# Stick-breaking fill by block count, the second recurrence's values projected before the first recurrence's queries, first gate blocks after the second recurrence's inputs

## The chip, the cores and the metric

One NeuronCore of a Trainium2 chip runs the whole kernel. The metric is device time in microseconds of that core, from start to end of one execution. Five engines work side by side: PE (TensorE, the matmuls), DVE (VectorE), ACT (ScalarE), POOL (GpSimd) and SP (SyncE, which here only issues DMAs). Each engine takes its own instructions strictly in order, and waits on semaphores where it needs another engine's result.

## What is computed

One decoder layer over 1024 tokens of width 1024. A projection `x @ w_in` yields the inputs of three causal mixers, each 256 wide with 4 heads: A, stick-breaking attention; B, a gated linear recurrence (HGRN2); C, another (GLA). Their outputs are normed, gated, projected up, weighted by sigmoid gates, summed, projected once more and layer-normed.

```python
# A: stick-breaking, per head, blocks of 128 queries against all keys before them
z = q @ k.T * scale
log_one_minus = where(s < t, log_sigmoid(-z), 0)
tail = reverse_cumsum(log_one_minus) - log_one_minus
a_out = masked_exp(s < t, log_sigmoid(z) + tail) @ v
# B and C: S_t = diag(f_t) S_{t-1} + k_t^T v_t ; o_t = S_t^T q_t
# merge
merged = sum_n sigmoid(x @ w_gate[n]) * (y[n] @ w_up[n])
out = layer_norm(ALPHA * x + merged @ w_out)
```

## The kernel before

All matmuls take their operands split into a high and a low part, so each product is three passes. A projection of 128 output channels over half of the tokens (`proj_T`, L207) is 24 matmuls with 512 columns; a projection of 256 channels for 128 tokens (`proj_N`, L220) is 24 matmuls with 256 columns.

The program is written as **chains** and a **stream**. Five chains run one after the other, and each is a long sequence of dependent small steps: the two stick-breaking units `c_sb(0)` and `c_sb(1)` (two heads each), then `c_rec` for GLA, for HGRN heads 0 and 1 (`("H", 0)`), and for heads 2 and 3 (`("H", 1)`). The stream is an ordered list of generators with all the plain projections, which depend on little. After each step a chain yields a number, which is added to a budget; the loop then draws pieces of the stream (each piece says what it costs, mostly 1.3 for six 512-column matmuls or twelve 256-column ones) until the budget is used up. Before a chain starts, `need(label)` draws whatever the chain still lacks, without any chain step between. A generator whose input does not exist yet yields 0.0, and that ends the drawing for this step: so `f_split(0)` (`ys0`) blocks the stream until the second stick-breaking unit has ended, and `f_finish(C_G, ...)` (`("y", 2)`) blocks it until the GLA chain has ended.

**Stick-breaking.** A unit has 24 chunks, each 128 queries against 1 to 4 blocks of 128 keys, 72 blocks in all. `weights` (L548) does two matmuls, two sigmoids on ACT, masks on POOL, a scan (L570) and a product (L571) on DVE. Three chunks later `transposed` (L577) turns the result over on PE (L586) and splits it (`ath` on ACT, `atl` on DVE, helper lines L98 and L99); `values` (L594) multiplies with V (L608). After `weights` and after `transposed` the unit yields `SB_T * 0.5`, which is 0.8 for a chunk of any width.

**Recurrence.** `c_rec` starts with small products (L645), fills of the score tiles `sc` on POOL (L662) and then seven levels h = 1 to 64, each for two halves of the tokens. In the GLA chain a half of a level copies Q into block-diagonal form (ACT, L675), takes its low part (DVE, L678, 8 instructions), splits K (tile `Kp`), does 12 matmuls (L694), copies the masked scores (DVE L703, up to h = 16; ACT after that; level 1 uses L670) and scales Q and K (DVE, L716 and L717). It yields `R4_T` = 3.4 per half of a level. After the levels come transposes of K (`kn`), the states (L745 to L753), the outputs (L765, L767, tiles `og`) and the norms (to L782).

**Stream pieces that matter here.** `f_cv` (`fC`), `f_ag` and `f_ck` project GLA's values, the gate of A and GLA's keys. `f_cq` (`GLA`) projects GLA's queries and multiplies them out on DVE and ACT (L406 to L409: the product, its three bf16 parts `prod`). `f_hi` (`vH`, L324) projects the values of both HGRN chains: eight `proj_N` and two ACT copies each, into four tiles. `f_h(0)` projects forget gate and queries of the first HGRN chain, 96 matmuls, with DVE work like that of `f_cq` (L419 to L437). `f_gate(0, True, 0, 2)` (`g0`) does the first two of eight gate blocks of branch A: per block and half 24 matmuls, a sigmoid into a `gt` tile, 6 matmuls with `ys0`'s split `yh`, `yl` (L505) and one DVE product into a tile `mT` (L508).

**Order of execution.** The program order is a priority, not the order on the engines. A scheduler lays out each engine's queue ahead of time: it takes the earliest instruction in program order whose inputs, by its own estimates, are there and whose output tile has a free buffer. Tiles come from pools with a fixed number of buffers; the ones here are `h` (29 buffers of 128x512 f32: `V`, `ks`, `kl`, `qs`, `vC`, `vH`, `K`, `Q`, `prod`, `yh`, `yl`, `mT`, `og` and others), `gt` (2: `gt`, the products before their split) and in PSUM `mm` (3, for all projections). A projection whose result has no free tile to go to keeps its `mm` buffer.

Of the kernel before, what the change touches and what calls it, by code (L numbers as in the profile page):

```python
# [32 lines left out]
PX = -3000000  # L33
NWO = 2
NWARM = 10
SB_T = 1.6
CV_T = 10.0
CV0 = 1
CV1 = 2
# [4 lines left out]
SB_LAG = 3  # L44
# [11 lines left out]
def hybrid_layer_kernel(ctx, tc, x, x_t, w_in, gla_gate_w2, gla_gate_b, hgrn_lb_logits,  # L56
# [276 lines left out]
    def f_cv():  # L333
        load_small()
        ws = load_w(W, C_V, 256, extra=C_R)
        vC = [H("vC", shape=[P, 2, 256]) for _ in range(4)]
        cr = sm.tile([P, 8, 16], F32, tag="cr", name="cr", bufs=1)
        for tt in range(8):
            pt = yield from proj_N(ws, tt, 272)
            nc.scalar.copy(vC[tt // 2][:, tt % 2, :], pt[:, 0:256])  # L340
            nc.vector.tensor_copy(cr[:, tt, :], pt[:, 256:272])
            yield 1.4
        d["vC"] = vC
        fs, xbs, nas = [[H(n) for _ in range(2)] for n in ("f", "xb", "na")]
        crT = [GT("crT", F32R) for _ in range(2)]

        def rank16():
            for th in range(2):
                c = crT[th]
                nc.gpsimd.memset(c[0:80].bitcast(F32), 0.0)  # L350
                pt = ptr()
                for j in range(4):
                    nc.tensor.transpose(pt[0:16, j * P:(j + 1) * P], cr[:, th * 4 + j, :], ident)
                nc.scalar.copy(c[0:16], pt[0:16])
                nc.vector.tensor_tensor(c[32:48], pt[0:16], c.bitcast(F32)[0:16], op=ALU.subtract)
                nc.scalar.copy(c[64:80], pt[0:16])
            later.append([CV1, up])

        def up():
            for th in range(2):  # L360
                xb, na = xbs[th], nas[th]
                pt = ptr()
                mm(pt, w2s[0:80], crT[th][0:80], start=True, stop=True)
                nc.vector.tensor_scalar(xb, pt, gb, None, op0=ALU.add)
                nc.vector.scalar_tensor_tensor(na, xb, -1.0, xb, op0=ALU.mult, op1=ALU.min)
                nc.vector.tensor_scalar(xb, xb, 0.0, None, op0=ALU.min)
            later.append([CV2, decay])

        def decay():

            lower_bound()
            with at_priority(PW):
                for na, xb in zip(nas, xbs):
                    nc.scalar.activation(xb, xb, AF.Exp, scale=1.0 / 16)
                    nc.scalar.activation(na, na, AF.Exp)
                for na in nas:
                    nc.scalar.activation(na, na, AF.Ln, bias=1.0)
                for na in nas:
                    nc.scalar.activation(na, na, AF.Exp, scale=-1.0 / 16)
            for th in range(2):  # L380
                nc.vector.tensor_tensor(fs[th], xbs[th], nas[th], op=ALU.mult)
            d["fC"] = fs
            budget[0] += CV_T

        later.append([CV0, rank16])

    def f_ck():
        uk = load_w(W, C_QK + P, P)
        K = [H("K") for _ in range(2)]
        for th in range(2):  # L390
            pt = yield from proj_T(uk, th)
            nc.scalar.copy(K[th], pt)
            yield 1.3
        d["KC"] = K
# [141 lines left out]
    def c_sb(un):  # L536
        qs, ks, kl = d["qk", un]
        V = d["V"][un]
        oT = [H("oT") for _ in range(2)]
        chunks = []  # L540
        for hd in range(2):
            for jp in range(4):
                for g in reversed(range((2 * jp + 5) // 4)):
                    for ti in range(2):
                        chunks.append((hd, jp, g, ti))
        right, part, at, po = {}, {}, {}, {}

        def weights(c):  # L548

            hd, jp, g, ti = c  # L550
            i = jp * 2 + ti
            ni = min(4, i + 1 - 4 * g)
            cw = ni * P
            cm = max(cw, 256)
            last = 4 * g + ni == i + 1
            qq, th = qs[hd][i // 4], slice((i % 4) * P, (i % 4 + 1) * P)
            be, om = R("be"), R("om")
            pt = pz()
            mm(pt[:, 0:cm], qq[:, th], ks[hd][g][:, 0:cm], start=True, stop=False)
            mm(pt[:, 0:cm], qq[:, th], kl[hd][g][:, 0:cm], start=False, stop=True)  # L560
            nc.scalar.activation(om[:, 0:cw], pt[:, 0:cw], AF.Sigmoid, scale=-0.125)  # L561
            nc.scalar.activation(be[:, 0:cw], pt[:, 0:cw], AF.Sigmoid, scale=0.125)
            if last:

                for a_, fill in ((om, 1.0), (be, 0.0)):
                    nc.gpsimd.affine_select(a_[:, cw - P:cw], a_[:, cw - P:cw], [[-1, P]], compare_op=ALU.is_gt, fill=fill,  # L566
                                            base=0, channel_multiplier=1)
            rv = om[:, 0:cw][:, ::-1]
            rt = right.get((hd, i))
            nc.vector.tensor_tensor_scan(rv, rv, rv, 1.0 if last else rt[:, 0:1], op0=ALU.mult, op1=ALU.bypass)  # L570
            nc.vector.tensor_tensor(be[:, 0:cw - 1], be[:, 0:cw - 1], om[:, 1:cw], op=ALU.mult)  # L571
            if not last:
                nc.vector.tensor_tensor(be[:, cw - 1:cw], be[:, cw - 1:cw], rt[:, 0:1], op=ALU.mult)
            right[hd, i] = om
            part[c] = (be, ni)

        def transposed(c):  # L577
            hd, jp, g, ti = c
            be, ni = part.pop(c)
            ns = min(4, 2 * jp + 2 - 4 * g)  # L580
            if ti == 0:
                at[hd, jp, g] = (S("ath", F32R, [P, 4, 256]), S("atl", F32R, [P, 4, 256]))
            ath, atl = at[hd, jp, g]
            pt = ptr([P, 4, P])
            for j in range(ni):
                nc.tensor.transpose(pt[:, j, :], be[:, j * P:(j + 1) * P], ident)  # L586
            ts = slice(ti * P, (ti + 1) * P)
            split(ath[:, 0:ni, ts], atl[:, 0:ni, ts], pt[:, 0:ni, :])
            if ni < ns:

                for a_ in (ath, atl):
                    nc.vector.tensor_scalar(a_[:, ni, ts], ident, 0.0, None, op0=ALU.mult)

        def values(c):  # L594
            hd, jp, g, ti = c
            if ti == 0:
                return
            hr, otr = ((rA, rB), (rB, rA))[hd]
            nst = 2 * jp + 2
            ns = min(4, nst - 4 * g)  # L600
            if 4 * g + ns == nst:
                po[hd, jp] = pav()[:, 0:256]
            p_ = po[hd, jp]
            at_ = at.pop((hd, jp, g))
            for s in range(ns):
                v = V[2 * g + s // 2][:, s % 2, hd, :]
                for n, a_ in enumerate(at_):
                    mm(p_, v, a_[:, s, :], start=(4 * g + ns == nst and s == 0 and n == 0), stop=(g == 0 and s == ns - 1 and n == 1))  # L608
            if g == 0:
                tmp = R("ot")  # L610
                sl = slice(jp % 2 * 256, jp % 2 * 256 + 256)
                nc.scalar.copy(tmp[hr, 0:256], p_[otr])
                nc.vector.tensor_tensor(oT[jp // 2][hr, sl], p_[hr], tmp[hr, 0:256], op=ALU.add)

        n = len(chunks)
        for k in range(n + SB_LAG + 1):
            if k < n:
                weights(chunks[k])
                yield SB_T * 0.5
            if 0 <= k - SB_LAG < n:  # L620
                transposed(chunks[k - SB_LAG])
                yield SB_T * 0.5
            if 0 <= k - SB_LAG - 1 < n:
                values(chunks[k - SB_LAG - 1])
        need(("ag", un))
        for th in range(2):
            nc.vector.tensor_tensor(oT[th], oT[th], d["ag", un][th], op=ALU.mult)
        d.setdefault("ya", []).append(oT)
        if un == 1:
            d["y", 0] = d["ya"]  # L630

    def c_rec(key, nh, V):
# [139 lines left out]
        for i, o in enumerate(og):  # L772
# [12 lines left out]


    stream = [("V", f_av()), (("qk", 0), f_qk(0)), (("qk", 1), f_qk(1)), (("ag", 0), f_ag(0)),
              ("fC", f_cv()), (("ag", 1), f_ag(1)), ("KC", f_ck()), ("GLA", f_cq()),
              (("ys", 0), f_split(0)), ("g0", f_gate(0, True, 0, 2)), ("vH", f_hi()), (("H", 0), f_h(0)),
              (("y", 2), f_finish(C_G, gng, "ogC", ("y", 2))), (("H", 1), f_h(1)), ("g0", f_gate(0, True, 2, 8)),  # L790
              (("y", 1), f_finish(H_G, hng, "ogH", ("y", 1))), (("ys", 2), f_split(2)), ("g2", f_gate(2, False)),
              (("ys", 1), f_split(1)), ("g1", f_gate(1, False, 0, 7)), ("wo", f_wout(range(NWO))), ("g1", f_gate(1, False, 7, 8))]
# [44 lines left out]
    for label, mk in chains:  # L837
        need(label)
        for t_fill in mk():
            budget[0] = max(budget[0], -3.0) + t_fill  # L840
            while budget[0] > 0:
                c = advance()
# [104 lines left out]
```

## Time and profile before

| | us |
|---|---|
| median of 3 runs (lowest, highest) | 838.28 (837.74, 839.07) |
| profiled execution | 838.19 |
| its span, first to last instruction | 836.3 |
| PE busy | 813.9 |
| DVE busy | 500.6 |
| ACT busy | 352.0 |
| POOL busy | 138.2 |

The profiled execution is 1.9 us longer than its span, and lies 0.1 us under the median. The two stick-breaking units run from 54 to about 129 and on to about 214 us, the GLA chain to about 335, the HGRN chains to about 455; gate blocks and the output projection fill the rest. A busy PE is not a PE at its peak, as matmuls overlap: six 512-column matmuls follow each other in 1.39 us though each shows some 0.4 us.

### The profile page before, as it was taken

The numbers are of one execution on the slowest core, as the hardware profiler recorded it, in microseconds if no ns is written. First come the engines' busy times: TensorE is split into PE (matmuls) and PEld (weight loads), VectorE is DVE, ScalarE is ACT, GpSimd is POOL, SyncE is SP. The second block draws the span as 40 slices with busy tenths as digits, with TensorE's granted clock in tenths as the row PEclk, the third lists the DMA queues.
The fourth block names the chain that finished last, engine by engine and source line by source line (L and its number), as shares of the span: only waits on it lengthen the run. The fifth ranks groups of instructions, "written<-read, shape, count | busy, mean of one in ns | idle before, by whom it ended". The sixth has DMA issues, their size and how long they took to land.

```text
span 836.3 us, 12346 instructions
## 1 busy us (share of the span) xinstructions
PE 813.9 (97%) x4576; PEld 694.8 (83%) x4576; DVE 500.6 (60%) x1033; ACT 352.0 (42%) x733; POOL 138.2 (17%) x234
## 2 busy tenths in 40 slices
PE   8999999999899999999999999999999999999996
PEld 7987799787779989988888889888888888888886
DVE  6469998869999868667844224222232223266665
ACT  6466565696544737455645213221222222241110
POOL 3011212131400012312110002222222121210000
PEclk9999999999999999999999999999999999999998
DMA  9421110110010101100412211121212122142211
GB/s 263 116 54 26 26 26 2 45 45 26 14 38 27 52 25 27 44 20 20 132 33 82 58 50 39 35 60 35 61 33 63 34 60 65 43 126 101 100 51 51
DMA packets 66508, 46.22 MB, mean 55 GB/s; under 512 B 4352, under 2 KB 61328, under 8 KB 66448
## 3 DMA queue, kind: packets, MB, share of 16 engines
q1 hardware_dynamic: 65008, 42.36, 18.2%
q10 hardware_dynamic: 1440, 3.08, 1.0%
q8 instruction: 36, 0.59, 0.3%
q14 instruction: 24, 0.20, 0.1%
HBM read 41.23 MB, written 4.19 MB: 54 GB/s over the span
## 4 chain that ended last, share of the span: by engine, by line
PE 80%; DVE 11%; issue 4%; ACT 2%; POOL 1%; DMA 1%; SPq 0%; POOLq 0%; DVEq 0%; ACTq 0%
PE mm L207 40%; PE mm L220 12%; PE mm L879 11%; PE mm L505 7%; PE z L694 4%; DVE om L570 2%; PE av L767 2%; DVE atl L99 1%; PE av L608 1%; DVE Qlo L678 1%; DVE be L571 1%; PE av L765 1%; DVE wl L99 1%; PE z L745 1%; DMA xraw<-in_x_t_dram 1%
## 5 line engine op out<-in xcount | busy, mean ns | idle before, releaser
L207 PE MATMUL mm<-xh,wh 128*128 128x512 f32 x576 | 230.3, 400 | 0.0
L207 PE MATMUL mm<-xh,wl 128*128 128x512 f32 x576 | 228.7, 397 | 0.0
L207 PE MATMUL mm<-xl,wh 128*128 128x512 f32 x576 | 227.7, 395 | 0.0
L207 PEld LDWEIGHTS mm<-xh,wh 128*128 128x128 f32 x576 | 109.4, 190 | 23.0 <-DVE mT L508 0.4
L207 PEld LDWEIGHTS mm<-xh,wl 128*128 128x128 f32 x576 | 108.2, 188 | 24.0
L207 PEld LDWEIGHTS mm<-xl,wh 128*128 128x128 f32 x576 | 108.5, 188 | 22.5
L99 DVE TENSOR_TENSOR wl<-wr,wh 128x512 fp32r<-128x512 f32 (+2 forms) x116 | 74.5, 649 | 80.6 <-ACT wh L98 79.4
L98 ACT CAST wh<-wr 128x512 fp32r<-128x512 f32 (+2 forms) x116 | 66.4, 576 | 105.4 <-PE mm L207 92.9
L220 PE MATMUL mm<-wh,xh 128*128 128x256 f32 (+1 forms) x320 | 92.0, 287 | 0.4 <-ACT wh L98 0.3
L220 PE MATMUL mm<-wl,xh 128*128 128x256 f32 (+1 forms) x320 | 90.9, 284 | 0.7 <-DVE wl L99 0.7
L220 PE MATMUL mm<-wh,xl 128*128 128x256 f32 (+1 forms) x320 | 90.5, 283 | 0.0
L879 PE MATMUL mm<-wo,mh 128*128 128x512 f32 (+1 forms) x288 | 80.8, 366 | 0.0
L511 POOL TENSOR_TENSOR mT<-mT,gt 128x512 f32<-128x512 f32 x32 | 46.8, 1463 | 178.9 <-DVE gt L510 178.9
L510 DVE TENSOR_TENSOR gt<-mm,gt 128x512 f32<-128x512 f32 x32 | 22.1, 691 | 83.2 <-PE mm L505 82.9
L499 ACT ACTIVATE gt<-mm 128x512 f32<-128x512 f32 x48 | 28.6, 596 | 97.1 <-PE mm L207 92.1
L220 PEld LDWEIGHTS mm<-wh,xh 128*128 128x128 f32 x320 | 60.4, 189 | 1.6 <-ACT wh L98 1.3
L220 PEld LDWEIGHTS mm<-wl,xh 128*128 128x128 f32 x320 | 60.3, 188 | 1.3 <-DVE wl L99 1.3
L220 PEld LDWEIGHTS mm<-wh,xl 128*128 128x128 f32 x320 | 60.4, 189 | 0.4 <-DVE xl L99 0.2
L879 PEld LDWEIGHTS mm<-wo,mh 128*128 128x128 f32 x288 | 52.0, 189 | 9.1 <-DVE wo L99 0.4
L879 PE MATMUL mm<-wo,ml 128*128 128x512 f32 (+1 forms) x144 | 52.6, 366 | 0.0
L505 PE MATMUL mm<-yl,wh 128*128 128x512 f32 x96 | 38.2, 398 | 1.9 <-DVE yl L99 1.9
L566 POOL TENSOR_SCALAR_AFFINE_SELECT om<-om 128x128 f32<-128x128 f32 x32 | 13.3, 414 | 151.3 <-ACT om L561 146.8
(204 smaller groups left out, 1318.5 us busy)
## 6 DMA issues: line engine op xcount, KB each, us to landing
wr<-in_w_in_dram SPq DMA_DIRECT2D x92, 256.0 KB, 2.8
xraw<-in_x_t_dram SPq DMA_DIRECT2D x16, 256.0 KB, 5.6
xr<-in_x_dram SPq DMA_DIRECT2D x8, 512.0 KB, 3.3
wr<-in_w_out_dram SPq DMA_DIRECT2D x16, 256.0 KB, 2.9
wr<-in_w_up_dram SPq DMA_DIRECT2D x24, 128.0 KB, 2.2
out_dram<-xr SPq DMA_DIRECT2D x7, 256.0 KB, 2.1
out_dram<-xr ACTq DMA_DIRECT2D x7, 256.0 KB, 2.1
lng<-in_ln_g_dram ACTq DMA_DIRECT2D x1, 512.0 KB, 4.3
```

Source lines behind the costliest of these rows:

```text
L98: nc.scalar.copy(hi, src)
L99: nc.vector.tensor_tensor(lo, src, hi.bitcast(F32), op=ALU.subtract)
L207: mm(pt, w_, x_, start=(n == 0), stop=(n == 23))
L220: mm(pt, x_, w_, start=(n == 0), stop=(n == 23))
L499: nc.scalar.activation(gt, pt, AF.Sigmoid)
L505: mm(pu, w_, y_[th], start=(k == 0), stop=(k == 5))
L510: nc.vector.tensor_tensor(gt, pu, gt, op=ALU.mult)
L511: nc.gpsimd.tensor_tensor(mT, mT, gt, op=ALU.add)
L570: nc.vector.tensor_tensor_scan(rv, rv, rv, 1.0 if last else rt[:, 0:1], op0=ALU.mult, op1=ALU.bypass)
L694: mm(pt[:, wi * nh:(wi + 1) * nh], k_[:, w * P:(w + 1) * P], q.rearrange("p a (n h) -> p a n h", h=h), start=(n == 0 and wi == 0), stop=(n ...
L767: mm(pt[:, wi, a, :], sc[b][:, wi, a, :], V(w)[:, a * 64:a * 64 + 64], start=(w == 0 and a == 0), stop=True, skip_group_check=True)
L879: mm(pt, l_, r_[e][:, o:o + w], start=(n == 0), stop=(n == 23))
```

## The change

Three edits. The stick-breaking yields become `SB_T * 0.5` times the number of key blocks of the chunk, with `SB_T` at 0.6 instead of 1.6: 0.3 to 1.2 per yield where it was 0.8. In the stream, `vH` moves from behind the first two gate blocks to ahead of `f_cq` (`GLA`). And the first two gate blocks move from ahead of `("H", 0)` to behind it. Nothing that is computed changes.

```diff
-SB_T = 1.6
+SB_T = 0.6
@@
+        def blocks(c):
+            hd, jp, g, ti = c
+            return min(4, jp * 2 + ti + 1 - 4 * g)
+
         def weights(c):
             hd, jp, g, ti = c
             i = jp * 2 + ti
-            ni = min(4, i + 1 - 4 * g)
+            ni = blocks(c)
@@
                 weights(chunks[k])
-                yield SB_T * 0.5
+                yield SB_T * 0.5 * blocks(chunks[k])
             if 0 <= k - SB_LAG < n:
                 transposed(chunks[k - SB_LAG])
-                yield SB_T * 0.5
+                yield SB_T * 0.5 * blocks(chunks[k - SB_LAG])
@@
     stream = [("V", f_av()), (("qk", 0), f_qk(0)), (("qk", 1), f_qk(1)), (("ag", 0), f_ag(0)),
-              ("fC", f_cv()), (("ag", 1), f_ag(1)), ("KC", f_ck()), ("GLA", f_cq()),
-              (("ys", 0), f_split(0)), ("g0", f_gate(0, True, 0, 2)), ("vH", f_hi()), (("H", 0), f_h(0)),
+              ("fC", f_cv()), (("ag", 1), f_ag(1)), ("KC", f_ck()), ("vH", f_hi()), ("GLA", f_cq()),
+              (("ys", 0), f_split(0)), (("H", 0), f_h(0)), ("g0", f_gate(0, True, 0, 2)),
               (("y", 2), f_finish(C_G, gng, "ogC", ("y", 2))), (("H", 1), f_h(1)), ("g0", f_gate(0, True, 2, 8)),
```

## Rows read from the trace of the kernel before

**Rows 1.** The page, part 1: engine, busy us, share of the span, instructions.

```profile
PE 813.9 (97%) x4576; PEld 694.8 (83%) x4576; DVE 500.6 (60%) x1033; ACT 352.0 (42%) x733; POOL 138.2 (17%) x234
```

**Rows 2.** Windows: stretch, length, then busy us of PE, PEld, DVE, ACT, POOL.

```profile
54.00:129.00 75.00, 71.42 (x425) 61.29 (x424) 68.34 (x130) 47.44 (x105) 13.39 (x32) 1.00 0.10 26
129.00:182.00 53.00, 51.26 (x316) 44.69 (x315) 43.65 (x84) 39.11 (x79) 12.63 (x28) 1.00 0.11 28
182.00:214.00 32.00, 29.74 (x158) 23.81 (x157) 29.94 (x66) 21.68 (x48) 7.20 (x16) 1.00 0.11 29
214.00:234.00 20.00, 18.05 (x129) 14.44 (x127) 19.83 (x33) 9.31 (x21) 7.06 (x8) 1.00 0.14 38
234.00:279.00 45.00, 42.32 (x313) 39.84 (x314) 43.40 (x123) 22.27 (x62) 3.11 (x10) 1.00 0.07 20
279.00:298.00 19.00, 19.00 (x112) 16.76 (x111) 11.77 (x31) 13.83 (x32) 2.66 (x5) 1.00 0.26 70
298.00:335.00 37.00, 36.73 (x281) 33.10 (x281) 30.72 (x75) 19.47 (x35) 8.55 (x15) 1.00 0.09 22
335.00:398.00 63.00, 63.00 (x416) 56.93 (x415) 42.91 (x94) 31.43 (x65) 15.32 (x31) 1.00 0.10 28
...
829.00:836.30 7.30, 0.00 (x0) 0.00 (x0) 3.54 (x10) 0.75 (x2) 1.50 (x2) 0.61 0.20 72
```

**Rows 3.** Who waited for whom, PE: us in total, times, longest.

```profile
PE av L608 <- DVE atl L99: 3.8, 5, 1.5
PE mm L505 <- DVE yl L99: 1.9, 1, 1.9
...
PE z L694 <- DVE sc L703: 1.4, 2, 1.0
...
PE z L694 <- DVE Kp L99: 1.2, 2, 0.8
```

**Rows 4.** The chain of work in order of time: start, us, what.

```profile
74.18 1.39 PE mm L207 x6
...
257.48 1.43 PE z L694 x12
258.91 4.24 PE mm L220 x36
```

**Rows 5.** Groups of DVE instructions by shape: busy us, mean ns of one, idle before.

```profile
L99 DVE TENSOR_TENSOR wl<-wr,wh 128x512 fp32r<-128x512 f32 x88 | 60.8, 698 | 59.1 <-ACT wh L98 58.0 <-PE mm L207 0.6
L703 DVE COPY_PREDICATED sc<-mask,z 128x512 f32<-128x512 int32 x32 | 26.9, 868 | 4.3 <-PE z L694 4.2
L678 DVE TENSOR_TENSOR Qlo<-Q,Qbd 32x128 fp32r<-32x128 f32 x96 | 24.6, 289 | 2.0 <-ACT Qbd L675 1.4
...
L716 DVE TENSOR_TENSOR Q<-Q,G 128x256 f32<-128x256 f32 x36 | 15.3, 430 | 4.4 <-ACT Qbd L675 2.0 <-POOL St L735 1.3 <-POOL G L719 1.0
...
L670 DVE COPY_PREDICATED sc<-mask,r 128x512 f32<-128x512 int32 x8 | 11.6, 1476 | 0.7 <-POOL sc L662 0.7
...
L434 DVE TENSOR_TENSOR Q<-mm,s 128x512 f32<-128x512 f32 x4 | 2.8, 690 | 1.4 <-PE mm L207 1.0 <-PE av L765 0.4
```

**Rows 6.** One line's instructions: ns min/median/max, first and last start.

```profile
L406 DVE SCALAR_TENSOR_TENSOR Q<-mm,f x2: 680/684/689, 192.9 to 206.4; 128x512 f32<-128x512 f32 x2
...
L694 PE MATMUL z<-Qbd,Kp x96: 277/283/386, 233.6 to 293.8; 128*128 128x256 f32 x96
```

**Rows 7.** Tile prod: what its engines waited for, who waited for it (us, times).

```profile
  PE av L767: 9.8, 2
...
  PE av L765: 7.1, 3
...
  DVE mT L508: 4.0, 1
```

## The prediction

> **What bounds the kernel now.** I read the page's first part, then windows cut at the chains' borders, then who waited for whom, then single lines. The page shows PE busy for 97% and DVE for 60% [rows 1], which suggests that only PE counts. The windows correct that [rows 2]. From 335 us on PE is full, with matmuls back to back (63.00 of 63.00 in the window shown), and the change can only shift that part. From 54 to 335 us DVE is nearly as full as PE: 68.3 of 75 in the first stick-breaking unit, 73.6 of 85 in the second (two windows), 63.2 of 65 from 214 to 279. PE's idle time there is the length less the busy time of each window: 3.6, 1.7, 2.3, 1.9, 2.7, 0 and 0.3, together 12.5 us. Nearly all of its longer waits are on DVE results: `atl` 3.8, `yl` 1.9, `sc` 1.4, `Kp` 1.2 us [rows 3]. Only this 12.5 us can be won; all matmuls stay. What can be lost is any further time in which the stream has nothing to give while DVE works through a chain.
>
> Prices on PE: six 512-column matmuls 1.39 us, 36 of 256 columns 4.24 us, the 12 matmuls of half a level 1.43 us [rows 4]. So `vH` (192 of 256 columns) is 22.6 us of PE, `("H", 0)` (96 of 512) 22.2, a gate half (30) 7.0 and the four halves moved 27.8.
>
> **Fill by width.** One unit's yields sum to 72 x 0.6 = 43.2 instead of 24 x 1.6 = 38.4: 4.8 units are some 5 us more of PE work in each, moved, not added. Narrow chunks draw 0.6 instead of 1.6, full ones 2.4. DVE's work per chunk (scan, product, `atl`) grows with width as well, so the draws now lie where PE waits for `atl`. But DVE is 91% full in the first unit, and cannot be outrun: of the 3.6 us idle I keep 2 (bounds 0, all covered, and 5, the same waits with the narrow chunks bare).
>
> **`vH` ahead of `f_cq`.** Before, the second unit's budget takes the rest of `fC`, `ag`, `KC` and `GLA`, and the stream then stands at `ys0` for the last six yields. The scheduler still found work, the matmuls of `g0` that need no `y`. After, budget 43.2 + 10 (`CV_T`) buys the rest of `fC` (7 pieces), `ag` (8), `KC` (8), all 16 of `vH` and 3 of the 8 pieces of `f_cq`. The other 5 are drawn by `need("GLA")`. `vH` loads DVE lightly: its copies are ACT's, and its four weight pieces cost DVE 4 x 0.70 [rows 5]. `f_cq` costs DVE nine instructions per half, at most 0.69 each by the nearest row (L434) [rows 5], and these leave the unit. So DVE gets room there and the unit is bound by PE; of 4.0 us idle (129 to 214) I keep 2 (bounds 0 and 4). Its DMAs, four weight pieces on SP's queue ahead of two, move earlier; SP waits for nothing there that PE lacks.
>
> The price is that `f_cq` ends later. Its last product starts at 206.4 now [rows 6]; after, at 206.4 + 22.6 less some 2 us of saved idle, about 227. Everything in the GLA chain hangs on it. What was ahead of the chain on DVE, however, is not all delayed with it.
>
> **The GLA chain.** Now 27.2 us pass from that product to the first L694, and 60.2 more to the last [rows 6]. Its own DVE work, by count: L678 24.6 (96 of them, all GLA's), L703 16 of 32, so 13.9, L670 4 x 1.48 = 5.9, Q scaled 14 x 0.43 = 6.0, K about the same, `Kp` 12 splits at about 0.43 (taken from the 256-column L716) 5.2: 62 us [rows 5]. That is why DVE shows 43.4 of 45. Between product and first L694, `atl`, `yl` and gate products crowd DVE now; after, the unit's tail is done by then, and 12 to 16 us should do: first L694 at 239 to 243. Then the levels: beside them DVE now has the gates' products, `vH`'s and part of `("H", 0)`'s work; after, `("H", 0)` comes first, whose halves cost DVE more (a forget half three instructions, a query half nine, some 7 to 8 us per half in all). So the 60 us do not shrink: last L694 some 6 us later than now, and the levels done near 305 instead of 298.
>
> **What PE has meanwhile.** From 227 to 305 are 78 us. PE has the levels (12 x 1.43 = 17.2) and the fill that comes ahead of the block at `("y", 2)`: 22.2 + 27.8. The chain asks for 6.0 + 14 x 3.4 = 53.6 units, the stream has 20.8 + 26.0 = 46.8, and from level 64 on nothing is drawn until the chain ends; before it had 67.6 and ran out only in the outputs. If all the fill can run, PE idles 78 - 67.2 = 11 us, or 3 if `("y", 2)` runs ahead into its three PSUM buffers (72 matmuls, 8.5 us). But the last stage (298 to 335 now, 0.3 us idle) then lacks this fill and idles up to 8 more: lower bound 11. If it cannot run, it is because tiles are short. In the levels `h` holds `vC` 4, `K` 2, `Q` 2, `vH` 4, `yh`/`yl` 8 and the f and K tiles of `("H", 0)` 4, which is 24; its first query half takes 5, and all 29 are gone. The second needs 3, and the gate block's `mT` more. Then each `mm` buffer is held by a result without a tile, and only 54 gate matmuls (12.5 us) still run: PE idles 78 - 17.2 - 22.2 - 12.5 = 26, with 2 us of new waits 28, the upper bound. That such waits exist the trace shows: `prod` waited for the outputs' matmuls 9.8 and 7.1 us, and an `mT` product waited 4.0 us for a matmul that reads `prod` [rows 7]. But there the fill was not stopped for long. I take 17 from 214 us to the end of the chain, near the middle, where 4.9 us stand now. The 1.9 us on `yl` are among those 4.9: with the gates later that wait is gone.
>
> **Sum.** Idle now 12.5; after 2 + 2 + 17 = 21. On the profiled execution's 838.2 (span 836.3, where the last window ends [rows 2], and 1.9 around it; 0.1 under the median): 838.2 + 8.5 = 846.7. Ends: 0 + 0 + 11 gives 836.7, 5 + 4 + 28 gives 862.7.
>
> The Trainium skill (Perfetto Trace Analysis, section Optimization Strategy) says that a gap which repeats on the engine that should be full can mean that no SBUF or PSUM is left for the next tile. By that rule the upper bound of the GLA chain would hold. The trace agrees only as far as the `prod` and `mT` waits go; a stretch of repeating gaps it does not show.
>
> **Rivals.** (1) Faster, about 830. The units' 7.6 us of idle and the 1.9 on `yl` go, and the chain is no later: DVE has some 15 us of room in the second unit and uses it for the unit's tail and the first half of `f_cq`, so that the levels keep their end at 298. Then idle falls from 12.5 to about 4: 838.2 - 8.5 = 829.7. It decides if the first L694 starts by about 233. For it: each wait that the trace names is met by one of the edits. Against: DVE was gapless from 234 to 279 and PE's fill there becomes dearer for DVE. (2) Tiles run out throughout: 2 + 2 + 28 instead of 12.5, 857.7; the mark is `mm` held while `h` is full. (3) The change doesn't do what it says: as the scheduler draws by readiness, the moves cancel and idle stays at 12.5: 838.2. For it: gate matmuls already ran ahead of `ys0`.
>
> **Chances.** Forecast (841 to 853) 0.45, rival 1 0.33, rival 2 0.12, rival 3 0.10. A measurement of this kernel can tell about 0.2% (1.7 us) from no change. Faster 0.33, same 0.11, slower 0.56. The range must reach rival 1 and the lower of rival 2: 829 to 857.
>
> **What would show it.** Right: windows of the units with PE idle under 3 us each; last L406 near 227, first L694 near 240, last near 300; PE idle over 10 us between there and the end of the GLA chain, and no wait of L505 on `yl`. Wrong: a first L694 at 233 or earlier; PE full from 227 to 305, which would say that DVE's list was shorter than I count; idle over 5 us in a unit, which would say that narrow chunks were left bare. From the end of the GLA chain on the two traces should agree instruction by instruction.

## The result, and the profile after

The changed kernel takes 866.8 us (862.1 to 867.2), the kernel before, on the same chip, 838.1: a ratio of 1.033 (95%: 1.031 to 1.035). The direction was forecast, the size was not: 8.5 us were expected and some 28 came, more than the range's upper end and more than rival 2. Its four executions lie further apart than those of the kernel before (837.7 to 839.1): 862.1 at a mean granted clock of 0.986, and 866.5 to 867.2 at 0.978 to 0.983. In `c_sb` and `c_rec` the changed kernel's lines stand 4 further down (L694 is L698, L608 is L612, L728 is L732); up to L546 nothing has moved.

The profiled execution is 866.5 us, its span 864.7. The page's first part and two digit rows of its second (the span in 40 slices of 21.6 us), to be held against [rows 1]:

```profile
span 864.7 us, 12344 instructions
PE 828.2 (96%) x4576; PEld 703.7 (81%) x4576; DVE 506.9 (59%) x1033; ACT 348.7 (40%) x729; POOL 137.2 (16%) x234
PE   8999999999879689999899999999999999999996
PEclk9999999999989699999999999999999999999999
```

PE's instructions are the same 4576, yet its busy time rose by 14.3 us. Half of the loss sits inside what counts as busy, and the length less the busy time doesn't show it. The other half is idle: span less busy was 22.4 and is 36.5, so 14.1 more, and 14.3 + 14.1 are the span's 28.4. The windows of [rows 2] in after, and one more (stretch, length, then busy us of PE, PEld, DVE, ACT, POOL, then granted clock, DMA share, GB/s):

```profile
54.00:129.00 75.00, 72.34 (x438) 62.67 (x437) 67.63 (x129) 47.98 (x105) 13.53 (x32) 1.00 0.10 26
129.00:182.00 53.00, 50.65 (x309) 43.79 (x308) 40.57 (x83) 38.83 (x76) 11.12 (x22) 1.00 0.14 37
182.00:214.00 32.00, 31.15 (x252) 30.42 (x251) 26.39 (x50) 19.78 (x53) 6.24 (x15) 1.00 0.03 7
214.00:234.00 20.00, 17.39 (x103) 14.01 (x101) 16.31 (x28) 8.50 (x20) 5.52 (x12) 1.00 0.22 59
234.00:279.00 45.00, 38.92 (x205) 30.54 (x204) 43.08 (x86) 20.02 (x44) 9.11 (x12) 0.92 0.10 27
279.00:298.00 19.00, 13.07 (x53) 10.12 (x52) 16.92 (x52) 7.84 (x21) 0.83 (x4) 0.67 0.00 1
298.00:335.00 37.00, 33.17 (x153) 26.81 (x154) 23.17 (x68) 17.68 (x40) 4.48 (x10) 0.89 0.09 24
335.00:398.00 63.00, 63.00 (x464) 57.83 (x463) 40.72 (x90) 28.20 (x54) 11.08 (x17) 1.00 0.13 33
398.00:460.00 62.00, 59.63 (x379) 51.18 (x378) 39.55 (x83) 28.56 (x60) 11.14 (x26) 1.00 0.20 62
```

PE's idle time by stretch is 2.7, 2.4 and 0.9 in the units (7.6 before), 2.6, 6.1, 5.9 and 3.8 from 214 to 335 (4.9 before), and a new 2.4 after 398. Look at 279 to 298: PE ran 112 matmuls there before and 53 now, at a granted clock of 0.67. The groups of PE by shape (busy us with overlaps counted once, mean ns, idle before) show whose busy time grew:

```profile
L698 PE MATMUL z<-Qbd,Kp 128*128 128x256 f32 x96 | 26.8, 377 | 15.0 <-DVE Kp L99 12.0 <-DVE sc L707 1.0 <-ACT sc L702 1.0
...
L698 PE MATMUL z<-Qlo,Kp 128*128 128x256 f32 x48 | 12.3, 348 | 0.0
```

The kernel before shows 16.2 and 9.6 for these two groups, so they account for 13.3 of the 14.3 us. A matmul with no neighbour to overlap with shows its whole length, and one at a lower granted clock takes longer: in the timeline below a pair of these matmuls shows 0.40 us at 282.07 and 0.63 us at 286.78. PE's timeline shows the stretch (start, us, what, and in brackets the idle time before it and its releaser):

```profile
278.28 0.39 PE L505 MATMUL mm<-yh,wh 128*128 128x512 f32 x1
...
280.02 0.40 PE L505 MATMUL mm<-yh,wl 128*128 128x512 f32 x1
281.49 0.51 PE L698 MATMUL z<-Qbd,Kp 128*128 128x256 f32 x2 [1.07 <-DVE Kp L99]
281.83 0.40 PE L698 MATMUL z<-Qlo,Kp 128*128 128x256 f32 x2
282.07 0.40 PE L698 MATMUL z<-Qbd,Kp 128*128 128x256 f32 x2
...
285.76 0.80 PE L698 MATMUL z<-Qbd,Kp 128*128 128x256 f32 x2 [1.63 <-DVE Kp L99]
286.35 0.63 PE L698 MATMUL z<-Qlo,Kp 128*128 128x256 f32 x2
286.78 0.63 PE L698 MATMUL z<-Qbd,Kp 128*128 128x256 f32 x2
...
290.76 0.80 PE L698 MATMUL z<-Qbd,Kp 128*128 128x256 f32 x2 [1.32 <-DVE Kp L99]
...
312.12 0.50 PE L207 MATMUL mm<-xh,wh 128*128 128x512 f32 x1 [0.30 <-DVE prod L435]
```

From 281.5 to 308.7 PE runs 80 L698 and nothing else, at first 12 in 5 us. Five times a half of a level waits for DVE's `Kp` (1.07 to 1.63 us); the last ones wait for ACT's copies of the scores. No stream piece runs between the last L505 at 280.0 and the L207 at 312.1. By then 504 L207 and 6 L505 had run since the start: 480 L207 are all that the stream lists ahead of the gates (the second half of `("H", 0)`'s queries among them), so 24 L207 and 6 L505 belong to the gates, and the gates then stood still.

What they stood for is on DVE. Its timeline where the stretch ends:

```profile
310.78 0.69 DVE L434 TENSOR_TENSOR Q<-mm,s 128x512 f32<-128x512 f32 x1 [0.91 <-PE tr L732]
311.38 0.68 DVE L435 TENSOR_TENSOR prod<-mm,s 128x512 f32<-128x512 f32 x1
...
327.08 0.69 DVE L508 TENSOR_TENSOR mT<-mm,gt 128x512 f32<-128x512 f32 x1 [5.85 <-PE tr L732]
```

L434 takes `("H", 0)`'s second query half out of its `mm` buffer. None of its inputs comes from L732, the transposes that read GLA's K, so what it waited for was the buffer of its result `Q`, which those reads set free; and the L207 at 312.1 waited for its `mm` buffer in turn. The first `mT` product, L508, waited for L732 as well. A second pool stood in the way: the 24 gate L207 had ended by 277.4, and ACT's first sigmoid on their result (L499) ran 40 us later, after L106 of the query half:

```profile
317.77 0.60 ACT L499 ACTIVATE gt<-mm 128x512 f32<-128x512 f32 x1 [0.22 <-DVE prod L106]
```

L106 works on the product that the query half keeps in the pool `gt`, and the sigmoid reads no result of it, so it waited for that buffer. The three `mm` buffers were held by the query half, which lacked a tile in `h`, by the gate's projection, which waited behind it for one in `gt`, and by the six L505, whose product L508 needs that sigmoid and an `mT`.

### The profile page after: what moved, and what is told of

Its sections match the earlier page's. It is cut to its first block, busy times and chain, and to the rows that moved or that the text cites. A ratio compares the mean times of both kernels' runs of the same rounds, so it can differ in the third digit from the quotient of the medians.

```text
span 864.7 us, 12344 instructions
## 1 busy us (share of the span) xinstructions
PE 828.2 (96%) x4576; PEld 703.7 (81%) x4576; DVE 506.9 (59%) x1033; ACT 348.7 (40%) x729; POOL 137.2 (16%) x234
## 4 chain that ended last, share of the span: by engine, by line
PE 80%; DVE 11%; ACT 4%; issue 2%; POOL 1%; DMA 1%; SPq 0%; POOLq 0%; DVEq 0%; ACTq 0%
PE mm L207 39%; PE mm L220 12%; PE mm L883 10%; PE mm L505 8%; PE z L698 3%; DVE Qlo L682 2%; PE av L612 2%; PE tr L590 1%; PE av L771 1%; ACT Qbd L679 1%; DVE wl L99 1%; DVE om L574 1%; PE av L769 1%; DVE sc L674 1%; PE z L564 1%
## 5 line engine op out<-in xcount | busy, mean ns | idle before, releaser
L207 PE MATMUL mm<-xh,wh 128*128 128x512 f32 x576 | 229.8, 399 | 1.6 <-DVE prod L435 1.4
L207 PE MATMUL mm<-xh,wl 128*128 128x512 f32 x576 | 229.5, 398 | 0.0
L207 PE MATMUL mm<-xl,wh 128*128 128x512 f32 x576 | 228.2, 396 | 0.0
L207 PEld LDWEIGHTS mm<-xh,wh 128*128 128x128 f32 x576 | 109.8, 191 | 25.1 <-DVE prod L435 1.6
L207 PEld LDWEIGHTS mm<-xh,wl 128*128 128x128 f32 x576 | 108.6, 189 | 24.0
L207 PEld LDWEIGHTS mm<-xl,wh 128*128 128x128 f32 x576 | 108.7, 189 | 23.2
L499 ACT ACTIVATE gt<-mm 128x512 f32<-128x512 f32 x48 | 28.6, 596 | 88.0 <-PE mm L207 83.8
L698 PE MATMUL z<-Qbd,Kp 128*128 128x256 f32 x96 | 26.8, 377 | 15.0 <-DVE Kp L99 12.0
L505 PE MATMUL mm<-yh,wh 128*128 128x512 f32 x96 | 38.6, 402 | 0.6 <-ACT gt L499 0.5
```

The lines of the kernel that those rows point to most:

```text
L207: mm(pt, w_, x_, start=(n == 0), stop=(n == 23))
L499: nc.scalar.activation(gt, pt, AF.Sigmoid)
L505: mm(pu, w_, y_[th], start=(k == 0), stop=(k == 5))
L698: mm(pt[:, wi * nh:(wi + 1) * nh], k_[:, w * P:(w + 1) * P], q.rearrange("p a (n h) -> p a n h", h=h), start=(n == 0 and wi == 0), stop=(n ...
```

## The experiments

Medians are given against the kernel before on the same chip. The theories: **tiles** (T where the expectations use a letter): the gates behind all of `("H", 0)` find no `h` buffer; **late queries** (L): `vH` ahead of `f_cq` delays the GLA chain; **surplus** (S): the larger sum of the width yields, carried over, puts pieces ahead of the levels; **clock** (C): the lower granted clock stretches the levels.

### The three edits one at a time

`e1_fill`, the first edit alone (called "width yields" below):

```diff
-SB_T = 1.6
+SB_T = 0.6
-                yield SB_T * 0.5
+                yield SB_T * 0.5 * blocks(chunks[k])
```

> The first edit alone: yields by block count with SB_T 0.6, the stream in its old order. Theory T (tiles: the loss comes from the gate blocks and the second query half of the first HGRN chain finding no free buffer in the pool h, so that PE stands bare through the GLA levels) and theory L (late queries: the loss comes from f_cq ending some 22 us later, with the fill used up before the chain is): both say no loss here, since neither move is made; 834 to 841 us, PE idle in the two stick-breaking units under 5 us together (7.6 before). A loss of 10 us or more would say that the fill by width itself is at fault.

844.1, ratio 1.008 (1.006 to 1.009), above the range that both theories gave. `e2_vh`, the move of `vH` alone:

```diff
-("KC", f_ck()), ("GLA", f_cq()), (("ys", 0), f_split(0)), ("g0", f_gate(0, True, 0, 2)), ("vH", f_hi()), (("H", 0), f_h(0)),
+("KC", f_ck()), ("vH", f_hi()), ("GLA", f_cq()), (("ys", 0), f_split(0)), ("g0", f_gate(0, True, 0, 2)), (("H", 0), f_h(0)),
```

> The second edit alone: vH ahead of f_cq, flat yields of 0.8, the first two gate blocks still ahead of the first HGRN chain's projections. In the order of the stream the gates get their four mT tiles before that chain's products ask for any. Theory T: the gate blocks run, PE has 27.8 us of them beside the levels, and only the query half of the HGRN projections is stopped; 838 to 848 us, and no long stretch of L694 alone at a low clock. Theory L: f_cq ends later than in the changed kernel (the flat budget buys only 12 of the 16 pieces of vH, so all of f_cq is drawn by need); 858 to 868 us.

849.3, ratio 1.014 (1.012 to 1.015), between the two ranges. The last L406 starts at 230.6, the first L694 at 246.3 (206.4 and 233.6 before). `e3_gates`, the move of the gates alone:

```diff
-(("ys", 0), f_split(0)), ("g0", f_gate(0, True, 0, 2)), ("vH", f_hi()), (("H", 0), f_h(0)),
+(("ys", 0), f_split(0)), ("vH", f_hi()), (("H", 0), f_h(0)), ("g0", f_gate(0, True, 0, 2)),
```

> The third edit alone: the first two gate blocks behind the first HGRN chain's projections, vH where it was (ahead of those), flat yields. f_cq ends where it did, near 206 us. Theory T: the pool h holds the same 24 tiles when the query half comes, the gates find none, and PE stands bare from there: 852 to 866 us, with a stretch of L694 alone at a granted clock under 0.8. Theory L: nothing is late: 834 to 842 us.

845.6, ratio 1.009 (1.007 to 1.010), less than the tile theory asked for. Its windows, busy us as above:

```profile
234.00:279.00 45.00, 40.96 (x238) 35.22 (x236) 42.51 (x107) 23.31 (x57) 3.09 (x10) 1.00 0.14 36
279.00:298.00 19.00, 18.05 (x101) 15.18 (x102) 18.60 (x58) 12.85 (x30) 1.80 (x5) 1.00 0.05 14
```

PE is still covered from 279 to 298. Here `vH`'s 22.6 us of PE lie behind `ys0` (147 of its 192 matmuls run from 214 to 279), so that 39 L207 are left for 279 to 298; in after `vH` has been spent in the second unit. So a shortage of tiles costs less while other work is left. Each edit alone costs time, 6.1, 11.2 and 7.5 us: together 24.8 of the 28.6.

### Tiles and late queries, crossed

`e4_split` is the whole change, but of `("H", 0)` only the forget half stays ahead of the gates; the queries, which take 5 and 3 `h` buffers, come behind them (`f_h` is cut in two for this, and only the stream's line is shown; the edit is against the changed kernel):

```diff
-(("ys", 0), f_split(0)), (("H", 0), f_h(0)), ("g0", f_gate(0, True, 0, 2)),
+(("ys", 0), f_split(0)), ("hf0", f_h(0)), ("g0", f_gate(0, True, 0, 2)), (("H", 0), f_hq(0)),
```

> All three edits, but the query half of the first HGRN chain's projections (48 matmuls with their products) goes behind the two gate blocks, the forget half stays ahead. So when the gates ask for their four mT tiles the pool h holds 24 of 29, not 29, while f_cq is as late as in the changed kernel and the sum of the fill is the same. Theory T: most of the 28 us comes back: 838 to 850 us, the gates' L505 run between the levels and the granted clock stays at 1.0. Theory L: 860 to 868 us as before this undo.

852.1, ratio 1.017 (1.016 to 1.019), between the two ranges: half of the loss is gone. The stretch is full again, and the first `mT` product (L513 there) starts at 267.5 instead of 327.1 and never waits for a transpose of K:

```profile
279.00:298.00 19.00, 18.75 (x105) 16.01 (x104) 18.66 (x56) 9.82 (x24) 2.24 (x5) 1.00 0.08 22
```

`e9_early` is the whole change with `f_cq` back ahead of `vH` (the edit is against the changed kernel):

```diff
-("KC", f_ck()), ("vH", f_hi()), ("GLA", f_cq()),
+("KC", f_ck()), ("GLA", f_cq()), ("vH", f_hi()),
```

> The changed kernel with f_cq ahead of vH again (vH stays ahead of ys0, the gates stay behind the first HGRN chain's projections, yields by block count). So f_cq ends near 200 us as in the kernel before, and only the order of gates and query half is that of the change. Theory T (tiles) and theory L (late queries) as two separate losses of about 14 us each: T alone is left, 850 to 858 us, with a stretch of L694 alone. If the two need each other (with early queries the levels end and free K before the fill runs into the full pool): 842 to 848 us, as with the third edit alone, which gave 845.6.

857.8, ratio 1.023 (1.022 to 1.025), in the range of T alone. The last L406 starts at 199.4, and the first L508 still waits for L732, 7.2 us in two waits. `e6_tail` has neither: width yields, `f_cq` early, `vH` behind it, gates ahead of `("H", 0)` (against `e1_fill`):

```diff
-(("ys", 0), f_split(0)), ("g0", f_gate(0, True, 0, 2)), ("vH", f_hi()), (("H", 0), f_h(0)),
+("vH", f_hi()), (("ys", 0), f_split(0)), ("g0", f_gate(0, True, 0, 2)), (("H", 0), f_h(0)),
```

> Yields by block count with SB_T 0.6; vH moved early too, but behind f_cq and ahead of ys0, gates ahead of the first HGRN chain's projections. So f_cq ends as early as in the kernel before, the second unit's last yields buy some nine pieces of vH instead of standing at ys0, and the gates get their tiles first. Theory L and S together: no late queries, no carried surplus, no wait of L505 on yl: 828 to 838 us, first L694 at 225 to 235. If fill that was spent early is missed at the end of the GLA chain (the stream runs dry 16 units before its end instead of 8): 838 to 845 us.

842.3, ratio 1.005 (1.004 to 1.007), in the upper of the two ranges. Over the kernel before (medians):

| | gates behind all of `("H", 0)` | gates ahead of its queries |
|---|---|---|
| `vH` ahead of `f_cq` | +28.6 (after) | +14.0 (`e4_split`) |
| `f_cq` ahead of `vH` | +19.7 (`e9_early`) | +4.5 (`e6_tail`) |

The order of gates and queries is worth 14.6 or 15.2 us, the late queries 9.0 or 9.5, and the two add up. (`e6_tail` has the gates ahead of the forget half too.) 4.5 us belong to neither. The traces show the late queries where a half of a level first needs the low part of Q: the first L698 on `Qlo` (L703 in `e4_split`) starts at 256.5 in after and 246.8 in `e9_early`, 258.1 in `e4_split` and 248.0 in `e6_tail`, some 10 us apart each time. With `f_cq` 34 to 37 us earlier the levels are only 10 us earlier, and the first score matmul of all hardly moves (248.7 and 246.3, 250.3 and 247.5).

### The buffers by themselves

`e11_h32` changes no order: it gives the pool `h` three more buffers, paid for with one of each weight buffer. `e12_h29` gives up the weight buffers alone and is its control.

```diff
-NWR = 4
-NHALF = 29
+NWR = 3
+NHALF = 32
-            wh = wp.tile([P, n, wt], F32R, tag="wh", name=nm("wh"), bufs=5)
-            wl = wp.tile([P, n, wt], F32R, tag="wl", name=nm("wl"), bufs=5)
+            wh = wp.tile([P, n, wt], F32R, tag="wh", name=nm("wh"), bufs=4)
+            wl = wp.tile([P, n, wt], F32R, tag="wl", name=nm("wl"), bufs=4)
```

> The changed kernel with 32 buffers in the pool h instead of 29, paid for by fewer weight buffers (wr 3 for 4, wh and wl 4 for 5). Three more buffers are what the second query half lacks; the gates' mT still find none, but two of three PSUM buffers come free, so some 30 to 60 gate matmuls more can run beside the levels. Theory T: 4 to 12 us under the next run in this list, which has the same weight buffers and 29. Otherwise the two agree within 2 us.

> The control to the run before it: the changed kernel with wr 3, wh and wl 4, and 29 buffers in h. Weights are drawn well ahead, so 864 to 872 us, near the changed kernel's 866.8.

With 32 buffers 855.2 (850.2 to 857.0), ratio 1.019 (1.016 to 1.023); with 29 buffers 866.4 (863.9 to 869.3), ratio 1.034 (1.030 to 1.037). The weight buffers cost nothing, the three tiles are worth 11.2 us, and each execution with 32 buffers is shorter than each with 29. The profiled executions (850.2 and 863.9) are the shortest of each. The window and line L508 (ns least, median, most; first and last start; what its idle time waited for), first with 32 buffers:

```profile
279.00:298.00 19.00, 16.96 (x92) 13.15 (x91) 18.10 (x56) 9.94 (x24) 0.88 (x4) 1.00 0.16 43
...
L508 DVE TENSOR_TENSOR mT<-mm,gt x16: 666/692/724, 311.7 to 506.7; 128x512 f32<-128x512 f32 x16
...
  PE tr L732: 1.4, 2
```

and with 29:

```profile
279.00:298.00 19.00, 12.79 (x50) 9.68 (x49) 17.34 (x53) 8.06 (x20) 0.85 (x4) 0.62 0.01 1
...
L508 DVE TENSOR_TENSOR mT<-mm,gt x16: 681/692/723, 323.9 to 518.2; 128x512 f32<-128x512 f32 x16
...
  PE tr L732: 5.6, 1
```

The first L508 starts 12.2 us earlier, the last one 11.5: the gain arises before the end of the GLA chain and stays. By the start of the bare run of L698 (297.1 and 278.6) the 32-buffer kernel has run 72 gate L207 and 12 L505, the control 24 and 6. These 54 matmuls are 12.5 us of PE at 1.39 for six [rows 4], about the gain. L434 waits for L732 in the control (1.1 us) and no longer with 32 buffers, and the first sigmoid of a gate (L499) runs at 276.4 instead of 314.9. So the tile theory is shown, by one pool size and a control that differs in nothing else. The three tiles give back 11.2 of the 28.6 us; with 32 buffers PE is bare again from 297.1. The rule of the Trainium skill cited in the prediction (Perfetto Trace Analysis, section Optimization Strategy) was the right reading for this part: in the stretch that the three tiles filled, 1.32 us gaps had repeated. The releaser named in each gap is DVE's `Kp`, though, and nothing in the gaps names a tile.

### Clock, surplus, and the yields

`e8_warm`: the changed kernel with 48 more matmuls on a tile of zeros, in levels 16 to 64, each ahead of the products that start the same PSUM tile afresh. They add work and change no value (against the changed kernel).

```diff
+                if parts and h >= 16:
+                    for _ in range(4):
+                        mm(pt.rearrange("p a n h -> p (a n h)"), wz[:, 0:P], wz, start=True, stop=True, skip_group_check=True)
```

> The changed kernel with idle matmuls added: in the GLA levels h = 16, 32 and 64, each score tile gets four bf16 matmuls of zeros (512 columns) before its own; they change no value and are 48 in all, some 10 us of PE at full clock. They lie in the stretch from 281 to 309 us in which PE has only L694 and the granted clock is 0.67. Theory C (the low clock is part of the loss, as each half of a level waits for its 12 matmuls at half speed): the clock in that stretch rises to 0.9 or more and the time falls by 3 to 8 us, to 858 to 863. If the clock costs nothing there, as DVE and ACT set the pace: 865 to 872 us.

866.4 (862.9 to 868.9), ratio 1.034 (1.031 to 1.037), as after, in the range given for a clock that costs nothing. The stretch in after, then in this kernel (one window each):

```profile
281.00:312.00 31.00, 22.41 (x96) 17.86 (x96) 27.45 (x87) 16.63 (x41) 2.07 (x7) 0.67 0.00 0
```

```profile
277.00:307.00 30.00, 24.96 (x131) 17.74 (x135) 28.31 (x91) 16.53 (x41) 2.85 (x8) 0.89 0.00 1
```

The granted clock rose from 0.67 to 0.89, and the stretch from the first bare score matmul to the next L207 stayed at 30.9 us (30.6 in after). DVE is busy for 27.45 of 31 us there, and the chain of waits from 276 to 314 us in after runs through DVE's L682 (28.3%) and ACT's L679 (22.7%) before PE's L698 (15.6%): these two set most of the pace.

The equal time doesn't show that the clock costs nothing, though. From wait to wait on `Kp` (PE's timeline in the section on the result), the half of a level that starts at 281.49 in after takes 4.27 us, at a granted clock of 0.97; the next three, up to 300.77, take 5.00, at 0.50, the lower level. Where the zeros have brought the clock back to 1.00, a half takes 4.26 us again:

```profile
291.71 0.50 PE L701 MATMUL z<-Qbd,Kp 128*128 128x256 f32 x2 [0.35 <-DVE Kp L99]
...
295.97 0.50 PE L701 MATMUL z<-Qbd,Kp 128*128 128x256 f32 x2 [0.35 <-DVE Kp L99]
```

So the lower clock costs 0.73 us a half, 2.2 us in those three. The zeros took as much: they stand in the chain of waits of this kernel from 274 to 312 us with 7.6%, 2.9 us, and from the last of these halves to the next L207 12.55 us pass instead of 11.35. The clock theory thus holds for some 2 us of the loss in those halves; what a higher clock would give without added matmuls is not shown. The Trainium skill (TensorE: Matmul & The Clock Gate, section HAM oscillation — how this bites in real kernels) describes the same course, a TensorE that falls to the lower clock in its gaps (waits for DMA there), and counts half of the time at that clock as lost. The trace agrees in kind; here 0.73 of 5.00 us was lost, as DVE and ACT shared the loop.

`e5_sum` is `e1_fill` with a smaller sum of yields (38.2 units in a unit, nearly the 38.4 of the flat ones; against `e1_fill`):

```diff
-SB_T = 0.6
+SB_T = 0.53
```

> As the first edit alone (yields by block count, old order of the stream), but with SB_T 0.53, so that one unit's yields sum to 38.2, as before (38.4), instead of 43.2. The first edit alone gave 844.1. Theory S (the sum: in the second unit the surplus finds the stream standing at ys0, is carried over, and puts 18 gate pieces at once ahead of the GLA chain's levels, whose first L694 starts at 247.5 instead of 233.6): the carry shrinks from 13.7 to about 4 to 5 units as in the kernel before, the first L694 returns to 232 to 238 and the time to 834 to 840 us. Theory W (the width itself: narrow chunks left bare, wide ones crowded): stays at 841 to 846 us.

843.0, ratio 1.006 (1.005 to 1.008), in the range of theory W, the width itself. The first score matmul moved from 247.5 to 237.5, but only 1.1 us came back: the units lost instead, with PE busy for 47.28 of 53 us from 129 to 182, where `e1_fill` shows 50.70. The surplus does put the levels later; what that costs by itself is not shown, as the smaller sum costs time in the units. `e10_unit0` has the width yields in the first unit alone (against `e1_fill`; the second yield is changed alike):

```diff
-                yield SB_T * 0.5 * blocks(chunks[k])
+                yield SB_T * 0.5 * blocks(chunks[k]) if un == 0 else 0.8
```

> The kernel before, with yields by block count (0.3 per block) in the first stick-breaking unit alone; the second keeps its flat 0.8, and the stream keeps its order. The first unit lost about 1.5 us less in waits with such yields. If that gain is real and the loss of the first edit alone sits in the second unit and the GLA chain: 835.5 to 838 us. If the 5 units more that the first unit draws only move the loss: 838 to 842.

846.7, ratio 1.010 (1.008 to 1.012): outside both expectations, and dearer than the edit in both units. PE's two longest waits there, in us, times, longest:

```profile
PE av L612 <- DVE atl L99: 3.6, 5, 1.6
PE z L563 <- ACT be L566: 2.7, 1, 2.7
```

It is lost in many places, 1 to 4 us per window of [rows 2], from the units to the HGRN chains. The scheduler lays out every queue anew when a yield changes, and I can't name one cause.

`e7_tail_flat` is `e6_tail` without the width yields: the kernel before with `vH` behind `f_cq` and ahead of `ys0` (against the kernel before).

```diff
-(("ys", 0), f_split(0)), ("g0", f_gate(0, True, 0, 2)), ("vH", f_hi()), (("H", 0), f_h(0)),
+("vH", f_hi()), (("ys", 0), f_split(0)), ("g0", f_gate(0, True, 0, 2)), (("H", 0), f_h(0)),
```

> The same order of the stream as the run before it in this list (vH behind f_cq and ahead of ys0), with the flat yields of 0.8 of the kernel before. The second unit's last six yields then buy three or four pieces of vH. Expected 833 to 838 us: the 1.9 us wait on yl and some of the 2.3 us idle from 182 to 214 go, nothing is added. If it beats the run by width, the larger sum does harm even with work to draw.

840.3, ratio 1.003 (1.002 to 1.004), above the expected range, yet 2.1 us under `e6_tail`: the wait on `yl` is gone, and another has come in its place:

```profile
PE z L694 <- DVE sc L703: 5.4, 3, 3.4
```

So of the 4.5 us that belong to neither of the crossed causes some 2.4 are `vH` ahead of `ys0` and 2.1 the width yields. No kernel beat the one before.

## Why the prediction was wrong in size

**Right: what the edits do.** `f_cq` came later (last L406 at 233.8), the wait of L505 on `yl` is gone, in neither unit is over 5 us idle, and PE's idle time lies where it was put, between the levels' start and the end of the GLA chain. Rows of single lines in after, as [rows 6]:

```profile
L406 DVE SCALAR_TENSOR_TENSOR Q<-mm,f x2: 691/692/693, 227.8 to 233.8; 128x512 f32<-128x512 f32 x2
...
L698 PE MATMUL z<-Qbd,Kp x96: 274/387/582, 248.7 to 326.1; 128*128 128x256 f32 x96
```

**The units: small error.** 2 + 2 us of idle were forecast, 2.7 + 3.2 measured.

**The step that failed: "I take 17 from 214 us to the end of the chain, near the middle".** The tile count beside it was right: 24 of 29 in use, 5 for the first query half, the second stuck. I then took the middle, because the waits of [rows 7] had not stopped the fill for long. The runs showed 31.8 us there in its place, worked out below. But in the kernel before the gates and `vH` lay beside the levels and gave PE other work, so those rows couldn't show what a shortage does without them (`e3_gates` has `vH` as cover and loses 7.5 us; `e9_early` has spent it and loses 15.2 by the same order of gates). Rival 2's condition held: `mm` was held while `h` was full, and through the query half's product the pool `gt` as well.

**Rival 2 itself was priced too low.** It let 54 gate matmuls run, 24 + 6 + 24 in three `mm` buffers. The second query half held one of the three, and the sigmoid that would have freed another waited for `gt`, so 30 ran. The prediction's own sum is then 78 - 17.2 - 22.2 - 7.0 (30 matmuls) = 31.6 instead of 26. Measured from 214 to 335: 18.4 us of idle and 13.3 us by which L698's busy time grew, 31.8 together, against 4.9. That the two agree to 0.2 us is partly luck, as the sum is over 227 to 305 us and the measurement over 214 to 335.

**A measure that misled.** Idle as length less busy time would have called the 17 nearly right, 18.4 measured. The levels were priced at 1.43 us per half, 17.2 in all, as in a full PE; bare, their groups show 13.3 us more. The sum of PE's idle time gives a loss only if the same matmuls show the same busy time. Some 2 us of the loss come with the lower clock (`e8_warm`), which the prediction leaves out.

**Milestones.** First L698 was forecast for 239 to 243 and came at 248.7, as `f_cq` ended 7 us later than forecast; the 14.9 us between its last product and that matmul are inside the 12 to 16. But "everything in the GLA chain hangs on it" is too strong: with `f_cq` 34 us earlier (`e9_early`) that matmul is 2.4 us earlier. Then PE waited 5.4 us, until 255.9, for `Kp`, with projections queued behind the waiting matmul; on DVE the level-1 copies (L674) and the forget half's L422 to L424 ran before it:

```profile
PE z L698 <- DVE Kp L99: 12.0, 6, 5.4
PE av L612 <- DVE atl L99: 2.8, 5, 1.1
PE av L612 <- DVE oT L617: 2.3, 1, 2.3
```

The levels' bare run ended at 308.7 instead of 305. The late queries are worth 9 us by the crossed runs; the prediction had 6 for the levels' delay, inside its 17. A count was off as well: a query half costs DVE seven instructions, 4.0 us in after, not nine, and with the forget half's three some 6 us, not 7 to 8.

**After the GLA chain the two traces were forecast to agree, and they do not**: 2.4 us are idle between 398 and 460, where the kernel before is full. Of the single edits only the move of `vH` does this: `e2_vh` is idle for 2.1 us there, `e1_fill` and `e3_gates` are full.

**Sum.** Units -1.7 (5.9 against 7.6), 214 to 335 +26.9 (31.8 against 4.9), after 398 +2.4, other busy time +1.0 (14.3 less 13.3): 28.6, against 28.4 of the span.

**Open.** Why width yields cost time in each form (+2.1 over `e7_tail_flat`, +6.1, +5.2 with the smaller sum, +8.6 in the first unit alone). And why the levels gain only 10 us from an `f_cq` that is 34 us earlier.

## What to carry to other kernels

Before a piece of a fill stream is moved, list which buffers are held at its new place, in every pool that it passes through (here `h`, `gt` and PSUM), and who frees them: a piece that finds no buffer doesn't merely come late, it holds PSUM and stops everything behind it. Fill that is moved into a stretch that is already nearly full is missing from the stretch it came from, and there it was the cover. Idle time read as length less busy undercounts whenever the same instructions run bare: compare the busy time of a group in both kernels too.

## What was unexpected of the hardware

A pair of 256-column matmuls takes 0.24 us from start to start at 281.8 and 0.43 at 286.4, after waits of 1.07, 0.41 and 1.63 us: the granted clock's two levels (2.4 and 1.2 GHz) in one chain. A half of a level, whose 12 matmuls then take 1.8 times as long, takes only 1.17 times as long (5.00 us instead of 4.27), as DVE and ACT have the larger part of the loop. One small difference has no explanation: the 2.3 us wait of L612 on `oT` in after's profile is missing in those of `e11_h32` and `e12_h29`, whose PE is busy for 20.00 of 20 us from 214 to 234, though the order there was not touched.
